# A hybrid attention and state-space encoder layer: where attention divides, where x is added, how q and k are normalized, and which token half the feed forward takes first

## The chip, the cores and the metric

The kernel runs on one core of a Trainium2 chip. The metric is the device time of one execution in microseconds (us). The kernel before took 2194.41, 2199.15 and 2200.61 us in three runs (median 2199.15).

## The reference

One encoder layer over 2048 tokens of width 1024, in float32:

```
h = rms_norm(x, norm1)
z = h @ w_in                      # 512 q, 128 k, 128 v, 512 u
q, k = rms_norm(q, q_gain), rms_norm(k, k_gain)     # over each head's 64 columns
scores = q k / sqrt(64) - slope * distance           # 128 tokens to either side
m = max(max(scores), sink);  p = exp(scores - m)
a = (p / (sum(p) + exp(sink - m))) @ v               # 8 heads, 2 kv heads
s = S5 state-space mixer of u, both directions, gelu, GLU
x = x + concat([a, s]) @ w_out
h = rms_norm(x, norm2)
out = x + square(relu(h @ w_ff1)) @ w_ff2            # 4096 wide
```

## The kernel before

Every large product is made of three TensorE matmuls of rounded high and low parts (`mm3`, L85 to L89: high × high, low × high, high × low), each 128 rows by 512 columns, into PSUM. PSUM has four tags of two banks each: `sc`, `ss`, `mm` for products and `tr` for transposes. Tokens are worked in 16 tiles of 128.

The stages, by the time in the profile: the projection of u and the set-up of the state-space part (to 134 us); the projection of q, k, v, tile by tile, with steps of the state-space part in between (to 350); attention, again with such steps (to 632, tail to 687); GLU and the output product's state-space half (to 873); the first feed-forward product (from 907 to about 1540); the second (to the end). Order in the text of the program is the programmer's; the framework's list scheduler then sets the order of instructions on each engine when the kernel is built, and each engine works its list strictly in order. All loads and stores are issued by one queue, SP, in order too.

*Norm of q and k* (`qkv_part`, L902). ScalarE squares (L918, L919), VectorE sums each of 10 heads' 64 columns (L924). Then the inverse root on 128x10 numbers: scaling (L925), ScalarE square root (L926), reciprocal (L927), one Newton step (L928 to L930, L932) and the factors `hsc` (L931). VectorE then multiplies q (L935) and twice k (L939).

*Attention* works in units: unit u is token tile n = u // 2 and kv head g = u % 2. `front(u)` makes scores and `softmax`; `back(u)`, `LEAD` units later, transposes the probabilities (`p_trans`), multiplies them with v (`pv`) and makes the attention half of the output product (`out_att`), whose result is added to x (L1100) and stored in `x1_dr`. The probabilities, 384 columns for each head, are multiplied with the reciprocal sums `rc` before they are transposed, two heads on VectorE (L1054) and two on ScalarE (L1056). S5 steps are VectorE's two-operand instructions of 512 columns (L564, L672, L675).

*Output, tiles 0 to 15* (`out_quarter`): for each tile, x1 is loaded (L1199), `out_ssm` makes two products of 512 columns (`pos`, 12 matmuls each) and adds them (L1211), x1 is stored, and `norm2` squares it on ScalarE (L1234), sums (L1235, L1236), raises to the power −1/2 on POOL (L1237) and scales it (L1238). For each pair of tiles four sums for a seven-product scheme (Strassen's) are made on POOL (L1249 to L1252), and seven pieces of 128x512 are stored in `hc_dr`.

*First feed-forward product*: 32 blocks, each seven products m = 1, 2, 6, 5, 7, 3, 4 of four `mm3`; blocks 0 to 15 take tokens 0 to 1023, blocks 16 to 31 the rest. The pieces of the token half are loaded back (`hs`, L1282), transposed (`pth`, L1292) and split into high and low (`hb`, L1293 on ScalarE, L1294 on VectorE). Weights are loaded (`w1r`, L1322), combined (L1329 to L1332) and split (`w1s`, L1338 on ScalarE, L1339 on POOL or VectorE).

Of the kernel before, what the change touches and what calls it, by code (L numbers as in the profile page):

```python
# [45 lines left out]
LEAD = 3  # L46
# [11 lines left out]
def hymba_kernel(ctx: ExitStack, tc: tile.TileContext, x, norm1, w_in, q_gain, k_gain, sink,  # L58
# [9 lines left out]

    ident = cst.tile([P, P], F32, name="ident")
    make_identity(nc, ident)  # L70
    mhalf = cst.tile([P, 16], F32, name="mhalf")
    nc.gpsimd.memset(mhalf, -0.5)

    ACT, DVE, POOL = nc.scalar, nc.vector, nc.gpsimd
    dist = cst.tile([P, 3 * P], F32, name="dist")
    nsink = cst.tile([P, NH], F32, name="nsink")
# [36 lines left out]
    v_all = att.tile([P, NT, NKV * HD], F32, name="v_all")  # L113

# [15 lines left out]
    rmag = sc.tile([P, NG], F32, name="rmag")  # L130
    dmask = sc.tile([P, GH], F32, name="dmask")
    dcol = sc.tile([64, NG // 2], F32, name="dcol")
# [267 lines left out]
    g1 = pw.tile([P, KD], F32, name="g1")  # L400
# [298 lines left out]
    def pair_out(i, h):  # L699
# [32 lines left out]
        ks = pm.tile([64, GH + C16 * GH], F32, tag="ks", name="ks")  # L732
# [154 lines left out]
    with tc.tile_pool(name="p1", bufs=2) as p1:  # L887
# [4 lines left out]
        DVE.tensor_tensor(gq[:, 0:1], gq[:, 0:1], gq[:, 1:2], op=ALU.mult)  # L892
        hsc = p1.tile([P, 10], F32, name="hsc", bufs=1)
        DVE.memset(hsc, 1.0)
        for h in range(NH):
            DVE.memset(hsc[:, h:h + 1], -1.0 / (SLOPE[h] * math.sqrt(HD)))
# [7 lines left out]
        def qkv_part(t):  # L904
# [18 lines left out]
            t3 = p1.tile([P, 10], F32, tag="t3", name="t3")  # L923
# [14 lines left out]
            for r in range(2):  # L938
                DVE.tensor_tensor(kd[:, :, r, :], pk3, rs3[:, 8:10].to_broadcast([P, 2, HD]), op=ALU.mult)  # L939
# [29 lines left out]
    with tc.tile_pool(name="pbq", bufs=2) as pbq, tc.tile_pool(name="pb", bufs=1) as pb, \  # L969
# [36 lines left out]
        mx_t = {}  # L1006
# [12 lines left out]
        def scores(n, g, h):  # L1019
# [3 lines left out]
            if h == 0:  # L1023
                p_t[n, g] = pbq.tile([P, GQ, 3 * P], F32, tag="p", name="p", bufs=LEAD + 1)
                mx_t[n, g] = pb2.tile([P, GQ], F32, tag="mx", name="mx")
# [7 lines left out]
                                     accum_out=mx_t[n, g][:, h:h + 1])  # L1033

        def softmax(n, g):
            lo, hi = keys(n)
            w = (hi - lo) * P
            mx, p = mx_t[n, g], p_t[n, g]
            ns = nsink[:, g * GQ:(g + 1) * GQ]
            nm = pb2.tile([P, GQ], F32, tag="nm", name="nm")  # L1040
            DVE.scalar_tensor_tensor(nm, mx, -1.0, ns, op0=ALU.mult, op1=ALU.min)
            es = pb2.tile([P, GQ], F32, tag="es", name="es")
            DVE.tensor_tensor(es, nm, ns, op=ALU.subtract)
            den = pb2.tile([P, GQ], F32, tag="den", name="den")
            for h in range(GQ):
                ACT.activation(out=p[:, h, 0:w], in_=p[:, h, 0:w], func=AF.Exp, bias=nm[:, h:h + 1],
                               accum_out=den[:, h:h + 1])
            ACT.activation(out=es, in_=es, func=AF.Exp)
            DVE.tensor_tensor(den, den, es, op=ALU.add)
            rc = pb2.tile([P, GQ], F32, tag="rc", name="rc")  # L1050
            DVE.reciprocal(rc, den)
# [33 lines left out]
        xr_t = {}  # L1085

        def out_att(n, half):
            if half == 0:
                xr = pb2.tile([P, D], F32, tag="xr", name="xr", bufs=1)
                nc.sync.dma_start(out=xr, in_=x2d[n * P:(n + 1) * P, :])  # L1090
                xr_t[n] = xr
            xr = xr_t[n]
# [20 lines left out]
        def front(u):  # L1113

            n, g = divmod(u, 2)
            for h in range(GQ):
# [4 lines left out]
                if h % 2 and u > 1 and wo_parts:  # L1121
# [13 lines left out]
        def back(u):  # L1135

            n, g = divmod(u, 2)
            if n < NT:
# [443 lines left out]
```

## Time and profile before

| | us |
|---|---|
| profiled execution | 2200.2 |
| its span | 2198.4 |
| runs | 2194.41, 2199.15, 2200.61 |
| TensorE busy | 2077.8 (95%) |
| VectorE busy | 1479.6 (67%) |
| ScalarE busy | 1016.0 (46%) |
| POOL busy | 590.3 (27%) |

PE is TensorE, DVE VectorE, ACT ScalarE, POOL GpSimd, SP the queue that issues transfers. A matmul counts as busy to its modelled end, and matmuls overlap, so the distance between starts is shorter than a row's duration. In 40 equal slices of the span TensorE's busy tenths are 7 in the first and one 5 near the middle of the feed forward, 9 in nearly all others; the granted clock has a 7 in the 17th and the 29th slice. The window table's columns are, after the window: its length; busy us and, in brackets, instructions of PE, of its weight loads, DVE, ACT and POOL; the mean granted clock of PE (1 is full); the share of its time that a DMA engine is busy; GB/s.

### The profile page before, as it was taken

The numbers are of one execution on the slowest core, as the hardware profiler recorded it, in microseconds if no ns is written. First come the engines' busy times: TensorE is split into PE (matmuls) and PEld (weight loads), VectorE is DVE, ScalarE is ACT, GpSimd is POOL, SyncE is SP. The second block draws the span as 40 slices with busy tenths as digits, with TensorE's granted clock in tenths as the row PEclk, the third lists the DMA queues.
The fourth block names the chain that finished last, engine by engine and source line by source line (L and its number), as shares of the span: only waits on it lengthen the run. The fifth ranks groups of instructions, "written<-read, shape, count | busy, mean of one in ns | idle before, by whom it ended". The sixth has DMA issues, their size and how long they took to land.

```text
span 2198.4 us, 30479 instructions
## 1 busy us (share of the span) xinstructions
PE 2077.8 (95%) x10546; PEld 1706.7 (78%) x10546; DVE 1479.6 (67%) x2806; ACT 1016.0 (46%) x2061; POOL 590.3 (27%) x451
## 2 busy tenths in 40 slices
PE   7999998999999997799999999999599999999999
PEld 7888886777767786688888788888487778778787
DVE  7959887998856644655445655554677776776765
ACT  4433336767666422455555655555342332333231
POOL 2000000000012223322332133221553663564441
PEclk9999999999999999799999999999799999999999
DMA  8925544333245448644445644442763443443344
GB/s 252 292 82 159 157 125 142 108 100 117 96 125 160 163 153 279 224 149 152 153 158 176 203 156 146 146 151 99 255 212 101 129 128 98 134 130 114 112 135 162
DMA packets 284394, 337.06 MB, mean 153 GB/s; under 512 B 62928, under 2 KB 211408, under 8 KB 284240
## 3 DMA queue, kind: packets, MB, share of 16 engines
q1 hardware_dynamic: 284240, 335.12, 46.9%
q8 instruction: 83, 1.36, 0.3%
q14 instruction: 71, 0.58, 0.1%
HBM read 206.11 MB, written 128.94 MB: 152 GB/s over the span
## 4 chain that ended last, share of the span: by engine, by line
PE 67%; DVE 13%; DMA 7%; POOL 5%; issue 3%; ACT 3%; SPq 1%; DVEq 0%; POOLq 0%; ACTq 0%
PE f L87 6%; PE f L89 6%; PE f L88 6%; PE f_al L89 5%; PE f_al L87 5%; PE f_al L88 5%; PE f_ga L87 3%; PE f_ga L89 3%; PE f_ga L88 3%; POOL w2s L1470 2%; PE pv L1075 1%; POOL fs L1496 1%; PE ptp L1065 1%; DVE acc L1541 1%; PE f_be L89 1%
## 5 line engine op out<-in xcount | busy, mean ns | idle before, releaser
L1541 DVE TENSOR_TENSOR acc<-f,acc 128x512 f32<-128x512 f32 x448 | 304.8, 687 | 164.6 <-PE f L89 158.0
L87 PE MATMUL f<-w2s,fs 128*128 128x512 f32 x896 | 352.9, 394 | 31.0 <-DVE acc L1541 15.7
L89 PE MATMUL f<-w2s,fs 128*128 128x512 f32 x896 | 351.4, 392 | 3.7 <-POOL fs L1496 3.7
L88 PE MATMUL f<-w2s,fs 128*128 128x512 f32 x896 | 351.3, 392 | 0.0
L1495 ACT ACTIVATE fs<-fr 128x512 fp32r<-128x512 f32 x224 | 141.6, 633 | 366.1 <-PE f L89 350.5
L1496 POOL TENSOR_TENSOR fs<-fr,fs 128x512 fp32r<-128x512 f32 x128 | 185.2, 1449 | 297.0 <-ACT fs L1495 255.8
L87 PEld LDWEIGHTS f<-w2s,fs 128*128 128x128 f32 x896 | 169.4, 189 | 74.1 <-ACT fs L1495 27.0
L1339 POOL TENSOR_TENSOR w1s<-w1r,w1s 128x512 fp32r<-128x512 f32 x96 | 135.2, 1409 | 311.9 <-ACT w1s L1338 303.0
L87 PE MATMUL f_al<-hb,w1s 128*128 128x512 f32 x512 | 201.0, 393 | 1.0 <-ACT w1s L1338 1.0
L89 PE MATMUL f_al<-hb,w1s 128*128 128x512 f32 x512 | 200.6, 392 | 1.1 <-DVE w1s L1339 0.9
L89 PEld LDWEIGHTS f<-w2s,fs 128*128 128x128 f32 x896 | 169.7, 189 | 40.3 <-POOL fs L1496 4.5
L88 PE MATMUL f_al<-hb,w1s 128*128 128x512 f32 x512 | 200.4, 391 | 0.0
L88 PEld LDWEIGHTS f<-w2s,fs 128*128 128x128 f32 x896 | 169.8, 190 | 34.7
L818 POOL TENSOR_TENSOR wgl<-wgr,wgh 128x512 fp32r<-128x512 f32 x8 | 10.4, 1311 | 521.0 <-DMA wgr<-in_w_glu_dram 508.2
L1339 DVE TENSOR_TENSOR w1s<-w1c,w1s 128x512 fp32r<-128x512 f32 x96 | 68.3, 711 | 88.0 <-ACT w1s L1338 88.0
L89 PEld LDWEIGHTS f_al<-hb,w1s 128*128 128x128 f32 x512 | 96.5, 189 | 22.0 <-DVE w1s L1339 1.3
L87 PEld LDWEIGHTS f_al<-hb,w1s 128*128 128x128 f32 x512 | 96.5, 189 | 21.3 <-ACT w1s L1338 1.4
L88 PEld LDWEIGHTS f_al<-hb,w1s 128*128 128x128 f32 x512 | 96.6, 189 | 19.6
L1338 ACT ACTIVATE w1s<-w1c 128x512 fp32r<-128x512 f32 x128 | 80.6, 630 | 49.7 <-PE f_al L89 48.4
L88 PE MATMUL f_ga<-hb,w1s 128*128 128x512 f32 x256 | 99.9, 390 | 0.0
L87 PE MATMUL f_ga<-hb,w1s 128*128 128x512 f32 x256 | 99.8, 390 | 0.0
L89 PE MATMUL f_ga<-hb,w1s 128*128 128x512 f32 x256 | 99.7, 389 | 0.0
(548 smaller groups left out, 4956.9 us busy)
## 6 DMA issues: line engine op xcount, KB each, us to landing
fr<-f_dr SPq DMA_DIRECT2D x224, 256.0 KB
w1r<-in_w_ff_dram SPq DMA_DIRECT2D x64, 512.0 KB
f_dr<-fs SPq DMA_DIRECT2D x128, 256.0 KB
f_dr<-f SPq DMA_DIRECT2D x96, 256.0 KB
w2r<-in_w_ff_dram SPq DMA_DIRECT2D x32, 512.0 KB
hs<-hc_dr SPq DMA_DIRECT2D x56, 256.0 KB
xt<-in_x_dram SPq DMA_DIRECT2D x16, 512.0 KB
q_dr<-qd SPq DMA_DIRECT2D x16, 512.0 KB
```

Of the source, the lines that this page charges most:

```text
L87: nc.tensor.matmul(ps_ap, lhsT=lh, rhs=rh, start=first, stop=False, skip_group_check=onto)
L88: nc.tensor.matmul(ps_ap, lhsT=lh, rhs=rl, start=False, stop=False, skip_group_check=onto)
L89: nc.tensor.matmul(ps_ap, lhsT=ll, rhs=rh, start=False, stop=last, skip_group_check=onto)
L818: eng_lo.tensor_tensor(lo, raw, hi, op=ALU.subtract)
L1065: nc.tensor.transpose(pt[:, h, :], p[:, h, kt * P:(kt + 1) * P], ident)
L1075: nc.tensor.matmul(po[g * HD:(g + 1) * HD, :], lhsT=v_all[:, lo + kt, g * HD:(g + 1) * HD], rhs=pT.pop((n, g, kt)), start=kt == 0, stop=kt ...
L1338: ACT.activation(out=t[:, 0], in_=src, func=AF.Copy)
L1339: (DVE if m in (6, 7, 3) else POOL).tensor_tensor(t[:, 1], src, t[:, 0], op=SUB)
L1470: (DVE if m in (6, 7, 3) and fp else POOL).tensor_tensor(t[:, 1], src, t[:, 0], op=SUB)
L1495: ACT.activation(out=t[:, 0], in_=src, func=AF.Copy)
L1496: (DVE if m in (6, 7, 3) else POOL).tensor_tensor(t[:, 1], src, t[:, 0], op=SUB)
L1541: DVE.tensor_tensor(a[:, cs], po, a[:, cs], op=ADD)
```

## The change

Seven edits. (1) Attention divides the product with v, not the probabilities: the reciprocal sums are copied to 64 columns each (`spread`), transposed on TensorE (`spread_t`, `ptr`) and multiplied into the product. The sums of both kv heads are handled at once. (2) The attention's product is stored without x; x is loaded and added when the tile is read for the state-space half (`load_xa`). (3) The inverse root of q and k is one power on POOL over 10 columns; its factors go into the scaling ahead of it. (4) The first feed-forward product begins with tokens 1024 to 2047, whose pieces are transposed straight from SBUF; only those of tokens 0 to 1023 go through `hc_dr`. Five of the last pair's seven pieces are transposed inside the first block. (5) LEAD is 2, not 3, and the output weights of the attention are split at three places in a unit, not two. (6) The squares of `norm2` go to PSUM; one of POOL's four sums goes to VectorE in the later half; the first block's weight splits are all on VectorE. (7) Small tiles are padded to 64 floats, and a tile of 24 floats is put in front.

```
-LEAD = 3
+LEAD = 2
...
+    cst.tile([P, 24], F32, name="offset")
...
+    def small(pool, n, rows=P, **kw):
+        return pool.tile([rows, 64], F32, **kw)[:, 0:n]
...
-            DVE.memset(hsc[:, h:h + 1], -1.0 / (SLOPE[h] * math.sqrt(HD)))
+            DVE.memset(hsc[:, h:h + 1], SLOPE[h] * SLOPE[h])
...
             DVE.tensor_reduce(ms, sq, axis=AX.X, op=ALU.add)
-            DVE.tensor_scalar(ms, ms, 1.0 / HD, EPS, op0=ALU.mult, op1=ALU.add)
-            ACT.activation(out=rs, in_=ms, func=AF.Sqrt)
-            DVE.reciprocal(rs, rs)
-            DVE.tensor_tensor(t3, rs, rs, op=ALU.mult)
-            DVE.tensor_tensor(t3, t3, ms, op=ALU.mult)
-            DVE.tensor_scalar(t3, t3, -0.5, 1.5, op0=ALU.mult, op1=ALU.add)
-            DVE.tensor_tensor(rs, rs, hsc, op=ALU.mult)
-            DVE.tensor_tensor(rs, rs, t3, op=ALU.mult)
+            DVE.scalar_tensor_tensor(ms, ms, HD * EPS, hsc, op0=ALU.add, op1=ALU.mult)
+            POOL.tensor_tensor(rs, ms, mhalf[:, 0:10], op=ALU.pow)
...
-            for r in range(2):
-                DVE.tensor_tensor(kd[:, :, r, :], pk3, rs3[:, 8:10].to_broadcast([P, 2, HD]), op=ALU.mult)
+            DVE.tensor_tensor(kd, pk[:, 0:128].rearrange("p (h o d) -> p h o d", o=1, d=HD).to_broadcast([P, 2, 2, HD]),
...
+        def spread(n):
+            rb_t[n] = pb.tile([P, GQ, NKV, HD], F32, tag="an", name="rb")
+            ACT.copy(rb_t[n], es_t[n].rearrange("p (g h o) -> p h g o", g=NKV, o=1).to_broadcast([P, GQ, NKV, HD]))
+
+        def spread_t(n):
+
+            pr_ = ps.tile([P, GQ, P], F32, tag="tr", name="ptr")
             for h in range(GQ):
-                if h < 2:
-                    DVE.tensor_scalar(p[:, h, 0:w], p[:, h, 0:w], rc[:, h:h + 1], None, op0=ALU.mult)
-                else:
-                    ACT.activation(out=p[:, h, 0:w], in_=p[:, h, 0:w], func=AF.Copy, scale=rc[:, h:h + 1])
+                nc.tensor.transpose(pr_[:, h, :], rb_t[n][:, h].rearrange("p g d -> p (g d)"), ident)
+            rT_t[n] = pr_
...
-            ACT.activation(out=ah, in_=pa3, func=AF.Copy)
-            DVE.tensor_tensor(al, pa3, ah, op=ALU.subtract)
+            ACT.copy(an, po.rearrange("p (h t) -> p h t", h=GQ))
+            DVE.tensor_tensor(an, an, rT_t.pop(n), op=ALU.mult)
+            ACT.activation(out=ah, in_=an, func=AF.Copy)
+            DVE.tensor_tensor(al, an, ah, op=ALU.subtract)
...
-            DVE.tensor_tensor(xr[:, cs], po, xr[:, cs], op=ALU.add)
-            if half == 1:
-                nc.sync.dma_start(out=x1_dr[n * P:(n + 1) * P, :], in_=xr)
+            xa = pb.tile([P, 512], F32, tag="xa", name="xa", bufs=2)
+            ACT.copy(xa, po)
+            nc.sync.dma_start(out=x1_dr[n * P:(n + 1) * P, cs], in_=xa)
...
+    def load_xa(n, bufs):
+
+        t = load_x1(n, po_, "x1", bufs)
+        xt = po_.tile([P, D], F32, tag="xx", name="xx", bufs=1)
+        nc.sync.dma_start(out=xt, in_=x2d[n * P:(n + 1) * P, :])
+        DVE.tensor_tensor(t, t, xt, op=ALU.add)
+        return t
...
-            junk = pn.tile([P, 512], F32, tag="junk", name="junk", bufs=1)
+            junk = ps.tile([P, 512], F32, tag="mm", name="junk")
...
-        POOL.tensor_tensor(t3, b22, b12, op=SUB)
+        (POOL if first else DVE).tensor_tensor(t3, b22, b12, op=SUB)
...
-    early = right_operands(0, [(m, i) for i in range(4) for m in PRODUCTS])
-    for n, _ in enumerate(out_quarter(3)):
-        if n > 0:
-            for _ in range(7):
-                next(early, None)
+    x1 = load_xa(NT // 2, 2)
+    pend = None
+    for n in range(NT // 2, NT):
+        nx = load_xa(n + 1, 2) if n + 1 < NT else None
+        out_ssm(n, x1)
+        if n == 11:
+            sb_stack.close()
+        nc.sync.dma_start(out=x1_dr[n * P:(n + 1) * P, :], in_=x1)
+        if pend is not None:
+            for m in PRODUCTS:
+                trans(m, (n - NT // 2) // 2 - 1, pend[m])
+        if n == NT - 1:
+            for j, m in enumerate((1, 2)):
+                trans(m, 3, h2_t[n - 1][:, j * 512:j * 512 + 512])
+        pend = norm2(n, x1)
+        x1 = nx
...
+            for m in PRODUCTS[2:6]:
+                trans(m, 3, pend[m])
+                after(next(blk))
+            trans(4, 3, pend[4])
```

On VectorE, in the projection of q, k, v, one tile's norm of q and k stands among S5 steps. Before, from the sum of squares to the split of q:

```order
L924 TENSOR_REDUCE msq<-sq 128x10
L564 TENSOR_TENSOR tmp<-bb_r,pv_n 128x512
L925 TENSOR_SCALAR msq<-msq 128x10
L564 TENSOR_TENSOR q_r<-c_r,pw_r 128x512
L564 TENSOR_TENSOR v<-v,tmp 128x512
L927 RECIPROCAL rsq<-rsq 128x10
L564 TENSOR_TENSOR tmp<-ta_s,tb_s 128x512
L928 TENSOR_TENSOR t_1977<-rsq 128x10
L564 TENSOR_TENSOR q_n<-c_n,pw_r 128x512
L929 TENSOR_TENSOR t_1977<-t_1977,msq 128x10
L931 TENSOR_TENSOR rsq<-rsq,hsc 128x10
L564 TENSOR_TENSOR t_c<-t_c,tmp 128x512
```

Now, the same tile:

```order
L931 TENSOR_REDUCE msq<-sq 128x10
L571 TENSOR_TENSOR tmp<-bb_r,pv_n 128x512
L932 SCALAR_TENSOR_TENSOR msq<-msq,hsc 128x10
L571 TENSOR_TENSOR q_r<-c_r,pw_r 128x512
L571 TENSOR_TENSOR v<-v,tmp 128x512
L936 TENSOR_TENSOR sq<-pq,rsq 128x512
L939 TENSOR_TENSOR kd<-pk,rsq 128x256
L571 TENSOR_TENSOR tmp<-ta_s,tb_s 128x512
L943 TENSOR_TENSOR qd<-sq,qd 128x8x64
```

The multiplication of q (L936) now stands two S5 steps behind the step that feeds POOL's power (L932), and seven small steps are one.

On SP, the queue of all transfers, in the output product's tiles 8 to 15. Before, `x` is a tile of the sum, `hc_dr` takes pieces for the first feed-forward product and `hs` are those loaded back:

```order
L1254 DMA hc_dr<-t_9277 128x512
L1199 DMA x_9289<-x_dr 128x1024
L1261 DMA x_dr<-x_9158 128x1024
L1282 DMA hs<-hc_dr 128x512 x4
L1261 DMA x_dr<-x_9289 128x1024
L1282 DMA hs<-hc_dr 128x512 x6
L1246 DMA hc_dr<-h_9383 128x512
L1282 DMA hs<-hc_dr 128x512 x4
```

Now, the last three tiles and what follows them (`xx` is a tile of the input x):

```order
L1229 DMA xx<-in_x_dram 128x1024
L1222 DMA x_9058<-x_dr 128x1024
L1350 DMA x_dr<-x_8965 128x1024
L1229 DMA xx<-in_x_dram 128x1024
L1222 DMA x_9109<-x_dr 128x1024
L1350 DMA x_dr<-x_9058 128x1024
L1350 DMA x_dr<-x_9109 128x1024
L1370 DMA w1r<-in_w_ff_dram 128x4x256 x6
```

No store to `hc_dr` and no load from it stands between the last eight tiles and the weights `w1r` any more; a load of the input stands with each tile.

## Rows read from the trace of the kernel before

**Rows 1.** Windows, stage by stage: columns as told above.
```profile
133.70:350.10 216.40, 202.51 (x1374) 175.06 (x1372) 195.48 (x450) 74.33 (x209) 1.11 (x11) 0.99 0.44 135
350.10:384.20 34.10, 26.29 (x157) 20.64 (x157) 24.52 (x87) 28.02 (x73) 0.00 (x0) 0.90 0.58 166
384.20:632.00 247.80, 242.88 (x1550) 186.24 (x1549) 212.11 (x581) 174.93 (x467) 0.00 (x0) 1.00 0.33 104
687.00:814.60 127.60, 123.36 (x529) 99.94 (x528) 70.78 (x95) 51.45 (x91) 35.79 (x30) 0.99 0.47 155
814.60:907.00 92.40, 69.06 (x306) 53.84 (x304) 43.56 (x70) 29.77 (x63) 24.93 (x24) 0.84 0.75 255
935.00:1182.00 247.00, 247.00 (x1092) 204.58 (x1091) 127.49 (x183) 137.51 (x234) 70.95 (x53) 1.00 0.45 152
```
**Rows 2.** Chain of waits to the feed forward: start us, us, what.
```profile
867.96 0.44 PE pth L1292 x4
868.87 0.23 PE pos__9407 L87
...
869.79 0.24 PE pos__9407 L89
...
871.07 6.49 DMA x<-x_dr
...
880.14 0.16 DVE ss L1236
...
880.44 0.56 POOL ss L1237
881.02 1.28 DVE h L1238
...
886.63 4.60 DMA hs<-hc_dr
...
893.71 0.42 SPq L1247
...
901.15 5.11 DMA w1r<-in_w_ff_dram
```
**Rows 3.** TensorE's timeline: start, us, instruction, count, idle before and releaser.
```profile
879.71 1.94 PE L1292 MATMUL pth<-ident,hs 128*128 128x128 f32 x8 [6.69 <-DMA hs<-hc_dr]
...
906.99 0.79 PE L87 MATMUL f_al<-hb,w1s 128*128 128x512 f32 x1 [1.03 <-ACT w1s L1338]
```
**Rows 4.** VectorE's groups, 137 to 348: count, busy us, mean ns, idle before.
```profile
L564 DVE TENSOR_TENSOR v<-bb_r,pv_r 128x512 f32<-128x512 f32 x10 | 6.8, 684 | 17.2 <-DMA u_dr<-ut 17.2
```
**Rows 5.** Chain of waits, 210 to 221 (VectorE bound): start, share, what.
```profile
215.28 0.08 DVE msq L925
...
215.96 0.13 DVE rsq L927
...
217.23 0.16 DVE t L929
...
217.97 0.17 DVE rsq L932
...
219.47 0.39 DVE kd L939 x2
219.86 0.40 DVE k_ll L950
```
**Rows 6.** Chain of waits, 830 to 857: a load of x.
```profile
851.01 4.55 DMA x<-x_dr
```
**Rows 7.** Timelines of VectorE and POOL, 829.5 to 837.5.
```profile
831.62 0.69 DVE L1211 TENSOR_TENSOR x<-pos__9032,x 128x512 f32<-128x512 f32 x1 [1.09 <-PE pos__9032 L89]
833.16 0.90 DVE L1235 TENSOR_TENSOR ss<-ss 128x1 f32<-128x1 f32 x1 [0.85 <-ACT junk L1234]
...
832.75 1.29 POOL L1251 TENSOR_TENSOR t<-h 128x512 f32<-128x512 f32 x1
```
**Rows 8.** VectorE's groups, 357 to 687.
```profile
L1054 DVE TENSOR_SCALAR p<-p,rc 128x384 f32<-128x384 f32 (+1 forms) x64 | 24.0, 416 | 0.4
```

More of the change, by code (lines that the diff above doesn't have):

```diff
@@ L113, in hymba_kernel @@
     v_all = att.tile([P, NT, NKV * HD], F32, name="v_all")
+    dist = att.tile([P, 3 * P], F32, name="dist")
+    nsink = small(att, NH, name="nsink")
     raw_h = att.tile([P, NKV * S], F32, tag="kh", name="raw_h")
@@ L129, in hymba_kernel @@
     tb_s = sc.tile([P, NG, 16], F32, name="tb_s")
-    rmag = sc.tile([P, NG], F32, name="rmag")
-    dmask = sc.tile([P, GH], F32, name="dmask")
-    dcol = sc.tile([64, NG // 2], F32, name="dcol")
+    rmag = small(sc, NG, name="rmag")
+    dmask = small(sc, GH, name="dmask")
+    dcol = small(sc, NG // 2, 64, name="dcol")
     KEEP, SCRATCH = 352, 1536
@@ L399, in hymba_kernel @@
     wql = pw.tile([P, KD, 768], F32R, name="wql")
-    g1 = pw.tile([P, KD], F32, name="g1")
+    g1 = small(pw, KD, name="g1")
     hstack = ExitStack()
@@ L1024, in scores @@
                 p_t[n, g] = pbq.tile([P, GQ, 3 * P], F32, tag="p", name="p", bufs=LEAD + 1)
-                mx_t[n, g] = pb2.tile([P, GQ], F32, tag="mx", name="mx")
+                if g == 0:
+                    for d, nm in ((mx_t, "mx"), (nm_t, "nm"), (den_t, "den"), (es_t, "es")):
+                        d[n] = pb2.tile([P, NH], F32, tag=nm, name=nm, bufs=3)
             qs = q_spl[n, g]
@@ L1120, in front @@
                 yield 0.33
-                if h % 2 and u > 1 and wo_parts:
+                if h and u > 1 and wo_parts:
                     split_wo(*wo_parts.pop(0))
@@ L1137, in back @@
             n, g = divmod(u, 2)
+            if g == 1 and n < NT:
+                sums(n)
             if n < NT:
@@ L1140, in back @@
                     p_trans(n, g, kt)
+                    if g == 1 and kt == 0:
+                        spread(n)
                     yield 0.44
@@ L1230, in norm2 @@
         h2_t[n] = h2
[L1231 removed]
+        ss = small(pn, 2, tag="ss2", name="ss2", bufs=2)
         for i in range(2):
[L1233 removed]
+            junk = ps.tile([P, 512], F32, tag="mm", name="junk")
             ACT.activation(out=junk, in_=x2[:, i * 512:i * 512 + 512], func=AF.Square, accum_out=ss[:, i:i + 1])
@@ L1245, in norm2 @@
         t4 = pn.tile([P, 512], F32, tag="t4", name="t4")
-        nc.sync.dma_start(out=hc_dr[n // 2, 1], in_=b11)
-        nc.sync.dma_start(out=hc_dr[n // 2, 2], in_=b21)
-        nc.sync.dma_start(out=hc_dr[n // 2, 3], in_=b22)
-        POOL.tensor_tensor(t3, b22, b12, op=SUB)
+        first = n < NT // 2
+        if first:
+            for m, t in ((1, b11), (2, b21), (3, b22)):
+                nc.sync.dma_start(out=hc_dr[n // 2, m], in_=t)
+        (POOL if first else DVE).tensor_tensor(t3, b22, b12, op=SUB)
         POOL.tensor_tensor(b12, b12, b11, op=SUB)
@@ L1252, in norm2 @@
         POOL.tensor_tensor(t4, b21, t2, op=SUB)
-        for m, t in ((5, b12), (6, t2), (7, t3), (4, t4)):
-            nc.sync.dma_start(out=hc_dr[n // 2, m], in_=t)
+        if first:
+            for m, t in ((5, b12), (6, t2), (7, t3), (4, t4)):
+                nc.sync.dma_start(out=hc_dr[n // 2, m], in_=t)
+        return {1: b11, 2: b21, 3: b22, 5: b12, 6: t2, 7: t3, 4: t4}
     def out_quarter(q):
-        x1 = load_x1(4 * q, po_, "x1", 2)
+        x1 = load_xa(4 * q, 2)
         for n in range(4 * q, 4 * q + 4):
-            nx = load_x1(n + 1, po_, "x1", 2) if n % 4 < 3 else None
+            nx = load_xa(n + 1, 2) if n % 4 < 3 else None
             out_ssm(n, x1)
@@ L1352, in keep @@
     def keep(g, m, t):
-        nc.sync.dma_start(out=f_dr[g % NFB, g // NFB, m], in_=t)
+        nc.sync.dma_start(out=f_dr[g % NFB, 1 - g // NFB, m], in_=t)
     def cell(tag, bufs=1):
-        return pf.tile([P, 512], F32, tag=tag, name=tag, bufs=bufs)
+        return pc.tile([P, 512], F32, tag=tag, name=tag, bufs=bufs)
     def ff1_block(g):
@@ L1408, in hymba_kernel @@
     load_w1(1)
+    left_w1(0, (1, 2))
+    for m in (1, 2):
+        split_w1(0, m)
     left_w1(0)
-    for m in PRODUCTS:
+    for m in PRODUCTS[2:]:
         split_w1(0, m)
@@ L1415, in hymba_kernel @@
         blk = ff1_block(g)
-        switch = right_operands(1, [(m, i) for m in PRODUCTS for i in range(4)]) if g == NFB - 1 else None
+        switch = right_operands(0, [(m, i) for m in PRODUCTS for i in range(4)]) if g == NFB - 1 else None
         def after(m, g=g, switch=switch):
@@ L1425, in hymba_kernel @@
         next(blk)
+        if g == 0:
+            next(blk)
         if g + 1 < NG1:
@@ L1433, in hymba_kernel @@
             load_w1(g + 2)
-        for _ in range(5):
-            after(next(blk))
+        if g == 0:
+            after(2)
+            for m in PRODUCTS[2:6]:
+                trans(m, 3, pend[m])
+                after(next(blk))
+            trans(4, 3, pend[4])
+            pnb_stack.close()
+            ph_ = d1_stack.enter_context(tc.tile_pool(name="ph_", bufs=1))
+        else:
+            for _ in range(5):
+                after(next(blk))
         last = (blk, after)
```

90 lines of the change are left out of this document (47 added, 43 removed).

## The prediction

> **What bounds the kernel now.** I read the window table first. Three kinds of stretch stand in it [rows 1]. In the feed forward TensorE is the bound without a gap: 1092 matmuls of 512 columns in 247.00 us, 0.2262 us each. In the attention (384.2 to 632) it is busy 242.88 of 247.80 us, with VectorE at 212 and ScalarE at 175. In the q, k, v projection (133.7 to 350.1) VectorE is the bound: 195.48 us busy of 216.40, and one row of its waits, 17.2 us for the load of u at the stretch's start [rows 4], fills nearly all of the rest; TensorE has 216.40 − 202.51 = 13.9 us idle, which is all that this stretch can give back.
>
> The weak place is between the attention and the feed forward. From 814.6 to 907 TensorE is busy 69.06 of 92.40 us at a mean granted clock of 0.84 [rows 1]; the output product's last matmul stands at 869.79 and the first feed-forward matmul at 906.99 [rows 2, 3]. The chain of waits says why [rows 2]: load of x (6.49 us), norm, store of its sums to HBM, load back (4.60), transposes, the issue (0.42) and landing of the next stores, load of w1 (5.11). One wait for the loads back is 6.69 us long on TensorE [rows 3].
>
> **The change part by part.** The sum is made against the profiled execution, 2200.2 us; its span is 2198.4. That is 1.05 us above the median 2199.15 of the runs shown, which I take off at the end. Minus is time saved.
>
> *Second half before first (814.6 to 907.0, 92.4 us).* Removed: the 28 stores and 28 loads of the half that comes first, and the queueing of x loads behind them. Added: for each of the 8 tiles a second load (the input x) and an addition over 1024 columns. None like it is in the rows; an addition of 512 takes 0.69 [rows 7] and the norm's product of 1024 takes 1.28 [rows 2], so I take 1.3. Work of a pair of tiles: TensorE 48 output matmuls × 0.233 (the mean of the 0.23 and 0.24 of [rows 2]) = 11.2 and 28 transposes × 0.11 (0.44 for four [rows 2]) = 3.1, so 14.3. VectorE: 2 × (1.3 + two additions 1.4 + small 0.3 + norm 1.28) + 7 subtractions of hb × 0.69 + one sum of 0.69 = 14.1. The buffer of x: two of them, so each carries every second tile through load 4.55 [rows 6], issue 0.42, the new addition 1.3, one addition 0.7, then from the load's landing to the end of the norm 4.7, which holds the other addition (877.56 to 882.30 [rows 2]): 11.7. VectorE and TensorE thus set about 14, and they wait on each other through two PSUM banks, which the squares of the norm now use as well. I take 15.5: 1.2 more for one handover of VectorE per tile, 0.6 each, about one more two-operand step of 512 columns (0.69 [rows 7]) ahead of the one awaited. Four pairs: 62. From the last output matmul to the first feed-forward one: w1's new tiles lie where the output weights lay, so their load cannot start earlier: a store's issue and its own, 0.42 each, load 5.11, copy to w1s and handovers about 1, 7.0; beside it the last addition and norm 4.7, eight transposes 0.9 to 1.94 [rows 3], and the copy and subtraction of hb 1.3, about 7.6. I take 7.6. Twenty transposes of the last pair are left over inside the first block: 2.2. Together 71.8 against 92.4: **−21**. Ends: pair at 14.1 and no further wait, −27; pair at 19 (rival 1), −6.6. The first feed-forward block now makes four subtractions on VectorE that POOL made; VectorE has half of that stretch free (127.49 of 247 [rows 1]), so nothing.
>
> *Norm of q and k (16 tiles).* Removed are a scaling, a ScalarE root, a reciprocal and five more steps on 10 columns. What a small step costs VectorE is its share of the chain, not its duration: 0.08, 0.13, 0.16 and 0.17 for the four shown, three more at 0.08 [rows 5], 0.78 in all. One step of 0.08 to 0.16 takes their place: 0.66 saved, 16 × 0.66 = 10.6. The two copies of k of 128 columns (0.39) become one of 256; the 256-column step in the rows takes 0.40: nothing. Added is a power on POOL. On one column it takes 0.56, and from the end of the step before it (880.30) to the norm that waits (881.02) 0.72 pass [rows 2]. In the new order one or two steps of 0.60 stand between, so between nothing and 0.72 is uncovered: 0 to 11.5, half is 5.8. Net **−5**. Lower end −13.9 (TensorE's idle time). Upper end: if ten columns cost ten times one, 5.6 per tile, less two covering steps 1.2, less 0.66 saved: 16 × 3.74 = +60 (rival 3). Queued behind the wait on VectorE is the whole S5 work of this stretch, and TensorE's products of it behind that.
>
> A row speaks against part of this: the small sum at 833.16 took 0.90 and ended when POOL's subtraction ended at 834.04, while the addition at 831.62, which reads PSUM, took its usual 0.69 beside POOL [rows 7]. The Trainium skill, SBUF — State Buffer, section "Who interferes with whom", says that a VectorE instruction with two SBUF inputs and a GpSimd one that reads SBUF exclude each other for a whole instruction; the trace agrees in these rows. By the rule each power would hold up VectorE for its 0.56 whatever stands between, 16 × 0.56 = 9.0, and this term would be −1.6 instead of −5.
>
> *Attention.* VectorE loses 64 scalings of 0.416 [rows 8], 32 additions of 0.69 and half of its small steps, and gains 16 products of 0.69: 26.6 + 22 − 11 = 38; ScalarE loses the other 64 scalings and gains 64 copies (two for each of 16 token blocks, 32 of the result), about as much. TensorE, the bound, gets 64 transposes × 0.11 = 7.0. Body: +7.0 from these, less what it waits for VectorE: 4.9 idle, and more that the table cannot show, as a matmul counts as busy to its modelled end. I take +1; ends +7 (nothing is waited for less) and −12 (half of VectorE's 38 us comes off, 19 − 7). Fill (350.1 to 384.2): 7.8 us idle, ScalarE 28.02 of 34.10; it loses its scalings and a table load, and one unit less is looked ahead: half, −4. Together **−3**, ends +7 and −16.
>
> *x added later, in tiles 0 to 7:* eight additions of 1.3 on VectorE, 70.78 busy of 127.60 [rows 1]: hidden; without that cover 10.4. The second load per tile, 4 MB, comes at a DMA share of 0.47: hidden.
>
> *Tiles moved onto a common grid of 256 bytes.* Output matmuls stand 0.233 apart, feed-forward ones of the same shape 0.2262 [rows 1, 2]. If the place of the operand is the reason, 192 matmuls of tiles 0 to 7 give 1.3, and the projections, whose operands move likewise, some 2: **−3**, ends 0 and −10.
>
> Feed forward from 935 on: TensorE without a gap, same matmuls: 0.
>
> Sum: −21 − 5 − 3 − 3 = −32; 2200.2 − 32 − 1 = **2167 us**.
>
> **Rivals.** (1) *The load chain or POOL sets the pace of tiles 8 to 15.* For it: loads of 4.55 and 6.49 us [rows 2, 6], and POOL's three sums of 1.3 and two powers of 0.56 per pair, 5.0, which hold up VectorE's two-SBUF steps [rows 7]: 14.1 + 5.0 = 19 a pair, the stretch 85.8, −6.6. Against: fewer transfers than now, and additions from PSUM are not held up. Time 2181 (2172 to 2194).
> (2) *The waits of TensorE on VectorE go with VectorE's work.* For it: in the attention VectorE has 38 us less of 212, and in the projection TensorE's 13.9 us idle are all its waiting on VectorE. Attention −16, projection −14, the other terms as above: 2145 (2137 to 2153). Against: TensorE at 98% busy there, with 7 us more to do.
> (3) *The power on ten columns is slow.* Place: POOL, once a tile, VectorE behind it. Price up to 5.6 us a tile, +60 where −5 stood: 2232. It eats the other 27 us from a power of 3.6 us on (3.6 − 1.2 − 0.66 = 1.74, × 16 = 28). For it: POOL's one power takes as long as 40% of a 512-column sum. Against: a 512-column sum at 1.29 is 2.5 ns a column, so that nearly all of the 0.56 seems to be a fixed cost.
>
> **How the numbers follow.** Forecast 0.55 (own range 2153 to 2175), rival 1 0.16, rival 2 0.19, rival 3 0.10. About 0.3% (6.6 us) is what a measurement of this kernel can tell from no change. Faster: 0.55 + 0.19 + 0.13 of rival 1 = 0.87; same: 0.03 of rival 1 and 0.03 of rival 3 = 0.06; slower: the rest of rival 3, 0.07. The range leaves out the slow end of rival 3 and the fast third of rival 2: 2140 to 2192.
>
> **What would show it.** Right: the first feed-forward matmul some 8 us after the last output matmul instead of 37 (869.79 to 906.99 [rows 2, 3]); pairs of tiles 8 to 15 near 15.5 us apart; a ten-column power below 0.8 us; VectorE's busy time in the projection some 10 us less, and that stretch about 5 shorter; attention within 4 us of 247.8; output matmuls 0.2262 apart; feed forward as long as before. Wrong: TensorE waiting for loads of x between tiles (rival 1), the attention shorter by 10 or more (rival 2), power rows of microseconds (rival 3); or, for the sum as a whole, transposes of the probabilities' divisors holding a PSUM bank for which other transposes wait.

## The result, and the profile after

The changed kernel takes 2231.05 us (median of 4 runs, 2229.08 to 2232.6) against 2199.8 before: a ratio of 1.0147, 95% interval 1.0129 to 1.0165: slower by 31 us. The forecast was 2167 and faster. The profiled execution of the changed kernel has a span of 2227.3 us.

The window table of the changed kernel, taken between the same events as before (columns as ahead of the prediction):

```profile
134.00:368.20 234.20, 207.12 (x1372) 179.14 (x1371) 185.93 (x338) 69.90 (x192) 36.90 (x27) 0.97 0.44 125
368.20:398.80 30.60, 25.53 (x149) 20.86 (x149) 20.72 (x63) 22.39 (x62) 0.00 (x0) 0.80 0.52 152
398.80:724.00 325.20, 308.81 (x1863) 225.80 (x1861) 217.09 (x539) 215.11 (x539) 13.83 (x10) 1.00 0.28 86
724.00:856.90 132.90, 126.49 (x534) 101.24 (x533) 80.61 (x103) 52.70 (x94) 39.27 (x30) 0.97 0.59 195
856.90:932.70 75.80, 59.86 (x293) 47.84 (x291) 53.35 (x79) 26.77 (x60) 21.36 (x20) 0.94 0.48 164
960.00:1207.00 247.00, 247.00 (x1092) 204.51 (x1091) 130.77 (x184) 137.64 (x234) 71.99 (x53) 1.00 0.45 154
```

and the row of before for the whole attention, from its first to its last output matmul, to set beside the third:

```profile
384.20:680.80 296.60, 287.07 (x1767) 216.53 (x1766) 238.97 (x637) 207.96 (x540) 11.70 (x9) 0.99 0.37 116
```

Read by length, stage for stage: the projection of q, k, v 216.4 to 234.2, although VectorE's busy time fell from 195.48 to 185.93 [rows 1]; the fill 34.1 to 30.6; the attention 296.6 to 325.2; tiles 0 to 7 133.8 to 132.9; tiles 8 to 15 and the way to the feed forward 92.4 to 75.8; the feed forward's matmuls as dense as before. So +18, −3, +29, −1, −17, and 3 in the rest: +29 in the traces.

**The projection.** One tile on VectorE, and POOL's instruction in it (start, us, instruction, idle before and releaser):

```profile
222.27 0.16 DVE L932 SCALAR_TENSOR_TENSOR msq<-msq,hsc 128x10 f32<-128x10 f32 x1
222.35 0.68 DVE L571 TENSOR_TENSOR x_i<-yi,t_c 128x512 f32<-128x512 f32 x1
224.88 0.69 DVE L936 TENSOR_TENSOR sq<-pq,rsq 128x512 f32<-128x512 f32 x1 [1.85 <-POOL rsq L933]
```

```profile
222.58 2.27 POOL L933 TENSOR_TENSOR rsq<-msq,mhalf 128x10 f32<-128x10 f32 x1 [15.64 <-DVE msq L932]
...
234.12 1.95 POOL L933 TENSOR_TENSOR rsq<-msq,mhalf 128x10 f32<-128x10 f32 x1 [9.27 <-DVE msq L932]
```

The power takes 1.95 us in the four tiles where no step of VectorE is in progress when it starts (the second row is one), 2.27 to 2.32 in the eleven where a step of 512 columns is, and 2.80 in the one where a step of 1.2 us is. The order shown ahead of the prediction, two S5 steps between L932 and L936, is that of the first tile alone: in eleven tiles one S5 step stands between, in four none. Then VectorE stands still, for 1.25 us in the first tile and 1.79 to 2.13 us in the others. Over the stage, by VectorE's waits (waited for: us in total, times, longest):

```profile
DVE sq L936 <- POOL rsq L933: 30.0, 16, 2.1
DVE v L571 <- DMA u_dr<-ut: 17.2, 1, 17.2
...
```

The second of these is as long before, and most of it lies ahead of the stage.

**The attention.** TensorE's waits with a releaser, of the changed kernel, then of before over the same stretch:

```profile
PE ptp L1079 <- ACT pT L1081: 7.5, 6, 1.8
PE pglu L92 <- ACT yh L854: 2.7, 1, 2.7
PE pkd L733 <- ACT xa L1113: 2.1, 1, 2.1
PE poa L92 <- ACT ah L1099: 2.1, 3, 1.1
...
```

```profile
PE pv L1075 <- DVE xr L1100: 3.9, 1, 3.9
PE ptp L1065 <- ACT pT L1067: 3.1, 4, 1.4
PE poa L89 <- DVE al L1082: 1.3, 2, 0.8
PE pkd L726 <- DVE xr L1100: 1.0, 1, 1.0
...
```

Before, most waits name VectorE (6 of 9.5 us); now they name ScalarE (15 of 16.4 us). VectorE lost 22 us of work in this stretch (238.97 to 217.09), ScalarE gained 7 (207.96 to 215.11). Of the 29 us that the stretch is longer, 7 are such waiting; TensorE's busy time grew by the other 22 (287.07 to 308.81), of which some 5 are GLU matmuls that were done in tiles 0 to 7 before.

**The way to the feed forward.** One wait holds most of what is left idle there, TensorE's for POOL's third sum of a pair:

```profile
PE pth L1329 <- POOL t L1284: 13.6, 4, 7.3
```

### The profile page after: what moved, and what is told of

It reads as the page before. It is cut to its first block, busy times and chain, and to the rows that moved or that the text cites. A ratio compares the mean times of both kernels' runs of the same rounds, so it can differ in the third digit from the quotient of the medians.

```text
span 2227.3 us, 30316 instructions
## 1 busy us (share of the span) xinstructions
PE 2092.9 (94%) x10610; PEld 1711.8 (77%) x10610; DVE 1460.6 (66%) x2590; ACT 1009.3 (45%) x2027; POOL 620.2 (28%) x459
## 4 chain that ended last, share of the span: by engine, by line
PE 44%; DVE 5%; POOL 4%; issue 2%; DMA 2%; ACT 0%; SPq 0%; DVEq 0%; POOLq 0%; ACTq 0%
PE f L92 6%; PE f L94 6%; PE f L93 6%; PE f_al L93 5%; PE f_al L92 5%; PE f_al L94 5%; PE f_ga L93 2%; POOL w2s L1535 2%; PE f_ga L94 2%; PE f_ga L92 2%; POOL fs L1561 2%; DVE acc L1606 1%; PE f_be L93 1%; PE f_be L94 1%; PE f_be L92 1%
## 5 line engine op out<-in xcount | busy, mean ns | idle before, releaser
L92 PE MATMUL f<-w2s,fs 128*128 128x512 f32 x896 | 353.0, 394 | 31.6 <-DVE acc L1606 16.6
L1390 POOL TENSOR_TENSOR w1s<-w1r,w1s 128x512 fp32r<-128x512 f32 x93 | 130.4, 1402 | 300.4 <-ACT w1s L1389 287.5
L1036 DVE CUSTOM_DVE_ANT_0 p<-pss,dist 128x384 f32<-128x384 f32 (+1 forms) x128 | 67.0, 537 | 63.4 <-PE pss L1035 59.7
L93 PE MATMUL f_ga<-hb,w1s 128*128 128x512 f32 x256 | 100.1, 391 | 1.5 <-DVE hb L1331 1.5
L92 PE MATMUL f_ga<-hb,w1s 128*128 128x512 f32 x256 | 99.9, 390 | 0.0
```

The lines of the kernel that those rows point to most:

```text
L92: nc.tensor.matmul(ps_ap, lhsT=lh, rhs=rh, start=first, stop=False, skip_group_check=onto)
L93: nc.tensor.matmul(ps_ap, lhsT=lh, rhs=rl, start=False, stop=False, skip_group_check=onto)
L1036: DVE.tensor_tensor_reduce(out=p_t[n, g][:, h, 0:w], in0=pss, in1=dist[:, off:off + w], scale=-SLOPE[g * GQ + h], scalar=-3.0e38, op0=ALU. ...
L1390: (DVE if m in (6, 7, 3) or g == 0 else POOL).tensor_tensor(t[:, 1], src, t[:, 0], op=SUB)
```

## The experiments

The stages are taken between the same events in each run: B is the projection of q, k, v; C the fill, the attention and tiles 0 to 7 together (work moves between these three: the changed kernel does some of the GLU's matmuls earlier); D tiles 8 to 15 up to the first feed-forward matmul; E the first feed-forward product from its first to its last matmul. Times are medians of the runs, stages us of the profiled execution.

| kernel | time | B | C | D | E |
|---|---|---|---|---|---|
| before | 2200 | 216.4 | 464.4 | 92.4 | 630.7 |
| changed | 2231.0 | 234.4 | 488.7 | 75.8 | 632.2 |
| 1 changed, norm undone | 2212.1 | 221.0 | 489.1 | 75.5 | 632.6 |
| 2 changed, division undone | 2221.2 | 233.8 | 481.6 | 78.7 | 631.1 |
| 3 changed, x undone | 2218.1 | 233.0 | 482.0 | 74.9 | 631.8 |
| 4 before, power alone | 2211.0 | 230.1 | 466.1 | 92.5 | 629.4 |
| 5 before, feed-forward order alone | 2202.4 | 217.2 | 467.6 | 74.6 | 648.0 |
| 6 changed, 1 to 3 together | 2192.4 | 217.8 | 473.5 | 74.6 | 629.8 |
| 7 as 1, with an idle power | 2212.0 | 219.5 | 489.6 | 76.4 | 630.4 |
| 8 changed, divisors in other bank | 2229.2 | 235.6 | 492.5 | 75.5 | 632.6 |
| 9 as 5, moved by 32 bytes | 2187.9 | 218.2 | 467.6 | 74.6 | 630.3 |
| 10 as 9, sums on VectorE | 2187.9 | 216.8 | 468.1 | 71.3 | 631.5 |
| 11 as 9, look-ahead 2 | 2192.5 | 219.4 | 473.1 | 74.7 | 630.1 |
| 12 changed, divisors not transposed | 2221.8 | 234.2 | 477.8 | 76.2 | 631.1 |
| 13 as 9, weights split at three places | 2192.0 | 218.5 | 470.4 | 74.6 | 632.0 |

**1. The norm undone.**

```
...
-            DVE.scalar_tensor_tensor(ms, ms, HD * EPS, hsc, op0=ALU.add, op1=ALU.mult)
-            POOL.tensor_tensor(rs, ms, mhalf[:, 0:10], op=ALU.pow)
+            DVE.tensor_scalar(ms, ms, 1.0 / HD, EPS, op0=ALU.mult, op1=ALU.add)
+            ACT.activation(out=rs, in_=ms, func=AF.Sqrt)
...
```

> The changed kernel with the norm of q and k made as before (square root on ScalarE, reciprocal, Newton step on VectorE), everything else changed. Theory 1: the ten-column power takes about 2 us and VectorE stands still for 1.9 of them in each of 16 tiles, 30 us, against 10 us of small steps saved: the projection of q, k, v goes back from 234 to about 216 us and the time from 2231 to about 2212. Rival 1: the projection is longer for another reason (the new places of the tiles, the order of the S5 steps); then it stays above 228 and the time above 2225.

Measured 2212.07, ratio to before 1.0054 (1.0039 to 1.0069): 19 us come back, 13 of them in B by the traces. Theory 1 holds for the time and not for all of the stage: B falls to 221.0, not to the 216 expected.

```profile
134.00:355.00 221.00, 205.59 (x1375) 178.76 (x1373) 195.22 (x434) 74.68 (x209) 1.11 (x11) 0.97 0.46 133
```

VectorE is as busy as before (195.22 us to 195.48), but idle for 5 us more, and TensorE's granted clock is 0.97 where it was 0.99. What makes these 5 us is not shown.

**4. The power alone.** The opposite edit, made in the kernel before.

> The kernel before with one part of the change alone: the norm of q and k by one power on POOL. Theory 1: 16 waits of 1.9 us on VectorE less 10 us of steps saved: about 2218, 18 to 20 above before. Rival 1: the wait appears only in the changed kernel's order; then 2190 to 2205.

Measured 2210.99, 1.0052 (1.0036 to 1.0069): +11, with B +13.6. The direction of theory 1, less than its size: by itself the power costs 11 us, within the changed kernel 19, and no run shows why these differ. VectorE waits as long here as in the changed kernel; the groups of VectorE and of POOL in this run:

```profile
L928 DVE TENSOR_TENSOR sq<-pq,rsq 128x512 f32<-128x512 f32 x16 | 11.1, 692 | 30.0 <-POOL rsq L925 30.0
```

```profile
L925 POOL TENSOR_TENSOR rsq<-msq,mhalf 128x10 f32<-128x10 f32 x16 | 35.8, 2236 | 188.3 <-DVE msq L924 178.3 <-DVE t L661 10.0
```

**7. The power without the wait.** The kernel of run 1, with one instruction more, whose result nobody reads:

```
             DVE.tensor_scalar(ms, ms, 1.0 / HD, EPS, op0=ALU.mult, op1=ALU.add)
+            xp = p1.tile([P, 10], F32, tag="xp", name="xp")
+            POOL.tensor_tensor(xp, ms, mhalf[:, 0:10], op=ALU.pow)
             ACT.activation(out=rs, in_=ms, func=AF.Sqrt)
```

> The changed kernel with the norm of q and k made as before, and POOL's ten-column power issued as well, its result unused. It tells waiting for the power apart from sharing a port with it. Theory 1: only the wait costs; the time is that of the kernel with the norm undone, 2212, within 4. Rival: the power holds up VectorE while it runs (1.95 us, 16 times); then 2220 or above.

Measured 2211.95, as without it (2212.07). POOL's power is as long, and VectorE's multiplication of q waits for nothing:

```profile
L935 POOL TENSOR_TENSOR xp<-msq,mhalf 128x10 f32<-128x10 f32 x16 | 35.9, 2242 | 177.9 <-DVE msq L933 167.9 <-DVE t L668 10.0
```

```profile
L945 DVE TENSOR_TENSOR sq<-pq,rsq 128x512 f32<-128x512 f32 x16 | 11.0, 686 | 0.5
```

Nor does the power hold up VectorE's other steps. One tile's power (start, us, instruction), and a step of VectorE with both inputs in SBUF that began and ended beside it:

```profile
173.77 2.26 POOL L935 TENSOR_TENSOR xp<-msq,mhalf 128x10 f32<-128x10 f32 x1 [10.73 <-DVE msq L933]
```

```profile
174.26 0.63 DVE L571 TENSOR_TENSOR tmp<-yr,t_s 128x512 f32<-128x512 f32 x1
```

In this run 15 such steps began while a power ran: 0.685 us in the median, the same as the others. Only the wait costs.

**2. The division undone.** `softmax` and the end of `pv` as before, for each kv head:

```
...
-            ACT.copy(an, po.rearrange("p (h t) -> p h t", h=GQ))
-            DVE.tensor_tensor(an, an, rT_t.pop(n), op=ALU.mult)
-            ACT.activation(out=ah, in_=an, func=AF.Copy)
-            DVE.tensor_tensor(al, an, ah, op=ALU.subtract)
+            ACT.activation(out=ah, in_=pa3, func=AF.Copy)
+            DVE.tensor_tensor(al, pa3, ah, op=ALU.subtract)
...
```

> The changed kernel with the probabilities divided before they are transposed, as before; look-ahead 2, x added later and the power stay. Theory 2: in the attention the 64 transposes of the divisors cost TensorE 8 us, and their PSUM bank and the two more copies on ScalarE make other transposes wait for some 10 more: the stretch from the first to the last attention output matmul goes from 325 to about 305 and the time from 2231 to about 2212. Rival 2: look-ahead 2 or the copies of the result on ScalarE make the waits; then only the 8 us of the transposes return and the time stays at 2221 or above. Rival 2b: more work on VectorE again makes it slower still, 2231 or above.

Measured 2221.18, 1.0093 (1.0075 to 1.0111): 10 us. The attention alone is 310.3, 15 shorter, but 5 of these are GLU matmuls that move back to tiles 0 to 7 and 3 stand in the fill; C keeps 7.1. Half of theory 2's gain, and by the expectation's own line it is rival 2's result, if only just (2221 was its edge): TensorE's 8 us and little more.

**12. The divisors not transposed.** `spread_t` gives the copy itself, in a buffer of its own, to the multiplication, so the attention's result is another one.

```
...
-            pr_ = ps.tile([P, GQ, P], F32, tag="tr", name="ptr")
-            for h in range(GQ):
-                nc.tensor.transpose(pr_[:, h, :], rb_t[n][:, h].rearrange("p g d -> p (g d)"), ident)
-            rT_t[n] = pr_
+            rT_t[n] = rb_t[n].rearrange("p h g d -> p h (g d)")
```

> The changed kernel without the 64 transposes of the divisors: the product is multiplied with the untransposed copy, so the attention's result is another one; all copies on ScalarE and the multiplication on VectorE stay. Theory 2: the attention falls by the 8 us of TensorE and a few of the waits for the bank, 2220 to 2224. Rival: the cost is in the longer chain of copies between the product and the next (ScalarE, VectorE, ScalarE, VectorE); then it falls by less than 4, to 2227 or above.

Measured 2221.82, 1.009 (1.0058 to 1.0121): 9 us, as much as undoing the whole division. The attention's row:

```profile
398.20:712.90 314.70, 300.36 (x1801) 218.63 (x1800) 212.47 (x531) 212.96 (x537) 13.24 (x10) 1.00 0.29 87
```

TensorE's busy time falls by 8.4 us, its idle time only from 16.4 to 14.3: the 64 transposes are the division's price mostly by their own time, and little by making others wait. What the copies and the longer chain cost is less than this can tell; the interval is 7 us to either side.

**8. The divisors in another bank.** `tag="tr"` becomes `tag="mm"` for `ptr`.

> The changed kernel with the transposed divisors in the PSUM tag of the output products, not in that of the transposes. Theory 2: the divisors hold a transposes' bank for up to 5 us while the next transposes wait; freed, TensorE's waits at the transposes of the probabilities fall from 8 us to below 4 and the attention by 5 to 10: 2221 to 2226. Rival: the transposes wait because ScalarE's copies stand behind its exponentials; then the time stays within 4 of 2231.

Measured 2229.18 (2226.98 to 2231.42), 1.0132 (1.0114 to 1.0149): within 4 us of 2231, as the rival says, and no different from the changed kernel that the runs can tell. TensorE's waits at the transposes of the probabilities did fall, from 7.5 to 2.0 us, but those at the output products rose from 2.1 to 6.4:

```profile
PE poa L92 <- ACT ah L1099: 6.4, 5, 1.9
PE ptp L1079 <- ACT pT L1081: 2.0, 4, 0.9
```

Both waits are for ScalarE; the bank changed which product waits. That the order of ScalarE's list makes them is read from these rows; no run changed that order alone.

**3. x undone.**

```
...
-            ACT.copy(xa, po)
-            nc.sync.dma_start(out=x1_dr[n * P:(n + 1) * P, cs], in_=xa)
+            DVE.tensor_tensor(xr[:, cs], po, xr[:, cs], op=ALU.add)
+            if half == 1:
+                nc.sync.dma_start(out=x1_dr[n * P:(n + 1) * P, :], in_=xr)
...
```

> The changed kernel with x added to the attention's output product on VectorE and stored whole, as before, and no second load in the later tiles. Theory 2: the attention stays within 5 us of 325, and tiles 0 to 15 of the output product gain 3 to 6 us from the additions and loads they lose: about 2226. Rival 3: the 32 copies of the result on ScalarE, in front of the copies that free the transposes' banks, make the attention's waits: then the attention falls by 10 or more and the time to 2215 or below.

Measured 2218.11, 1.0077 (1.0062 to 1.0092): 13 us, more than theory 2 gave. The attention falls by 3.4 (321.8), tiles 0 to 7 by 2.9, tiles 8 to 15 by 0.9, the projection by 1.4; 2 to 4 are spread over the rest. In C TensorE is idle 4 and busy 3 us less. Neither theory: a little everywhere, and by which way is not shown.

**5 and 9. The feed-forward order alone, and 32 bytes.** Everything but edits 4 and 6 as before, except that three small tiles have other places or sizes (`dist`, `nsink`, `ks`); then one line more:

```
+    cst.tile([P, 8], F32, name="offset")
     ident = cst.tile([P, P], F32, name="ident")
```

> The kernel before with one part of the change alone: the second token half first, its pieces transposed from SBUF, the squares in PSUM (look-ahead 3, probabilities divided, x added in the attention, norm of q and k as before, tiles not padded). Theory 4: this part saves by itself what the traces show between the last eight tiles' first output matmul and the first feed-forward one (92.4 to 75.8): about 17, less the loads of x that it does not need, 2181 to 2184. Rival 4: the gain needs the other parts, or is given back in the feed forward; 2192 or above.

> The kernel with the feed-forward order alone, with one tile of 8 floats put in front, which moves the left tiles by 32 bytes: the split weights w1s and the transposed tokens hb then have the same address modulo 256 (224; without it 192 and 224). Theory 5: the place of the two operands to each other sets the pace, 0.2262 us a matmul instead of 0.233, and the first feed-forward product falls from 648 to 631: 2183 to 2186. Rival 5: the slower pace comes from something else in that kernel; then it stays at 2202.

Measured 2202.41 (1.0005, 0.9994 to 1.0015), then 2187.87 (0.9941, 0.9918 to 0.9964). In the first, D gives 17.8 and E takes 17.3 back: in 247 us only 1061 matmuls pass. In the second, 1091. The windows, of 5 and of 9:

```profile
920.00:1167.00 247.00, 247.00 (x1061) 198.40 (x1059) 123.75 (x175) 133.24 (x227) 68.27 (x52) 1.00 0.45 151
```

```profile
920.00:1167.00 247.00, 247.00 (x1091) 204.66 (x1091) 130.88 (x185) 137.74 (x235) 71.36 (x52) 1.00 0.45 153
```

TensorE is busy all the time and at full clock in both; each matmul is 0.2328 or 0.2264 us. The one line moves tiles and does nothing else. In the built programs it changes where the weights stand to the tokens: addresses modulo 256 of 192 and 224 in 5, 224 and 224 in 9. So theory 5 holds, and it is the two together that count and not the one address: in kernel 5 the output matmuls, both operands at 192, follow each other every 0.227 us, before (224 and 32) every 0.234 (medians). Kernel 9 is faster than the kernel before and the changed one.

**6. Three parts undone.**

> The changed kernel with the norm, the division and the addition of x all made as before; look-ahead 2, the output weights split at three places, the padded tiles and the new feed-forward order stay. Theory: the three parts add up, 2231 less 19, 10 and 13 as each gave alone: 2189, and what stays above the kernel with the new feed-forward order alone is the look-ahead of 2, 5 to 10 us in the attention. Rival: look-ahead 2 costs nothing; then both kernels come out within 3 us.

Measured 2192.37, 0.9962 (0.9949 to 0.9975), 3 above the sum, as the theory says. It is 4.5 above kernel 9, which is not clear of the noise; C is 5.9 above that of kernel 9.

**11 and 13. Look-ahead 2, and the weights at three places.**

```
-LEAD = 3
+LEAD = 2
...
-                if h % 2 and u > 1 and wo_parts:
+                if h and u > 1 and wo_parts:
```

> The moved kernel with the feed-forward order alone, with look-ahead 2 and the output weights split at three places in a unit. Theory 6: look-ahead 2 shortens the fill by 3 us and costs the attention 8 to 12 by more changes between kinds of product and waits behind ScalarE: 4 to 9 us slower than with look-ahead 3. Rival 6: it costs nothing, within 2 us, and the 11 us that the attention keeps with all three parts undone come from the places of the tiles.

> The moved kernel with the feed-forward order alone, look-ahead 3 again, but the attention's output weights split at three places in a unit instead of two. It tells apart the two edits that the kernel with look-ahead 2 needed together. Theory 6: the look-ahead itself costs the 14 us of the attention; the time is that of the kernel without this edit, 2188, and the attention 296 to 299. Rival: the weights' splits, moved up in front of ScalarE's and VectorE's work of the first units, cost it; then the attention is 305 or more and the time 2191 or above.

Measured 2192.51 with both edits and 2191.95 with the second alone, both against 2187.87 (whose runs go from 2184.87 to 2192.58). By time the two cannot be told apart: the second alone has the time of its rival and the attention of theory 6. By the traces the attention is 310.3 with both and 299.0 with the second alone, against 296.4; the fill 28.8, 34.3 and 34.4. So look-ahead 2 lengthens the attention by 11 and gives 6 back in the fill and 3 in tiles 0 to 7: net 2.7 in C, beside 2.8 of the splits. With the same number of matmuls in C, TensorE is busy 444 us in kernel 9, 445 with the splits and 452 with look-ahead 2 as well, and idle 23, 25 and 21: look-ahead 2 saves waits and loses more in busy time. Changes between kinds of product (last section) go from 118 to 139 in C, which is about 2 of those us; the rest is not explained. That the expected 4 to 9 us belong to the look-ahead is not shown.

**10. POOL's sums on VectorE.** `POOL` becomes `POOL if first else DVE` for the other three sums of `norm2`.

> The same, and in the later token half the three sums that POOL still makes are made on VectorE. TensorE waits 13 us for POOL's sums there in the changed kernel. Theory: a sum takes 0.7 instead of 1.3 to 1.7 and the stretch before the feed forward falls by 4 to 8 us: 2177 to 2182. Rival: VectorE is the bound of these tiles and takes it back; within 3 us of the kernel without it.

Measured 2187.91: the rival. D falls by 3.3 in the trace, TensorE now waits for VectorE's sums (8.6 us where it waited 11.9 for POOL's), and the time is that of kernel 9, to the 5 us that these intervals leave open (0.9946, 0.9925 to 0.9967):

```profile
PE pth L1316 <- DVE t L1271: 8.6, 4, 6.1
```

## Why the prediction was wrong

It failed in three terms of its sum: the cover of the power, VectorE's relief set against TensorE's new work in the attention, and x's move, which it held to be hidden. The parts, as undoing them one by one priced them: norm 19 (11 when made alone, run 4), x 13, division 10, look-ahead and splits 5 (kernels 11 and 9), less 12 that the feed-forward order saves (kernel 9): +35, against +31 measured together.

**The norm (−5; B measured +18, of which undoing the norm returns 13 and the norm alone adds 14).** The saved small steps were right: 10.6 forecast, VectorE's busy time fell by 9.6. What failed is the cover: "between nothing and 0.72 is uncovered", from the row of a power over one column. Ten columns take 1.95 us and more instead of 0.56, at most one S5 step covers it in 15 of the 16 tiles, and 1.9 stay bare in the mean: 30.0. This is rival 3's mechanism and I had the upper end in hand, 5.6 a tile. I set it aside because a subtraction over 512 columns costs 2.5 ns a column; a power is another operation, and that row said nothing of it. By the rows now, 1.39 us for nine columns more are some 154 ns a column, an estimate. That rival 3's time, 2232, is the measured one is chance: at 2 us the power was below the 3.6 from which rival 3 alone would decide. The rule of the Trainium skill (SBUF — State Buffer, section "Who interferes with whom") would have put the term at −1.6, with VectorE held by each power. The traces agree in one direction only: a power issued while a step of VectorE ran took 2.27 instead of 1.95, so POOL was held; in run 7 VectorE's steps that began during a power took their usual 0.685 and were not.

**The attention and fill (−3, measured +25; +24 with tiles 0 to 7).** I booked 7 us of transposes and then let VectorE's relief pay for them: 38 us less work, of which 6 were to come back. The work fell by 22, and TensorE's waits for VectorE did fall, from 6 us to 1; but its waits for ScalarE rose from 3 to 15, so that nothing was paid. I had counted ScalarE's work ("about as much") and not where its copies now stand, between one product and the next. The transposes cost 9 of the time and 11 in C (run 12), the look-ahead and splits 5 together (run 11), and x's move cost 7 in C (run 3), which I had priced at nothing in the attention and "hidden" in tiles 0 to 7; all of it together was 13, and by which way is open. Another 3 in C come with the new feed-forward order, in tiles 0 to 7 (kernel 9), which I had not seen at all. That is 26 where the stages say +24. The forecast's last sentence named divisors that hold a PSUM bank; in run 8 another bank gave back 2 us, which is within the spread, so that place is not the cost.

**Tiles 8 to 15 (−21, measured −16.6).** Right in mechanism: 75.8 against 71.8. What is late next is not the load of x but POOL: transposes wait 13.6 us for its third sum (one of POOL's sums took 1.29 in [rows 7]; this one takes 1.51 on average now). From the last output matmul (921.8) to the first of the feed forward 10.9 us pass, not 8, of them 7.3 waiting for that sum. Run 10 shows that moving the sums to VectorE mostly moves the wait: 3.3 us less in D, none in the time.

**The places of the tiles (−3).** The rows had it, 0.233 against 0.2262 [rows 1, 2], and the output matmuls did go to 0.227; with tiles 0 to 7 only 0.9 shorter, the gain is not seen in the sum. But the size at stake was larger than my 10: E has 2688 matmuls, and with the feed-forward order alone, without edit 7, each was 0.0064 longer, 17 us (kernels 5 and 9). I had not asked what the new order does to the places of its own tiles.

**Two slips that changed nothing in the sum.** VectorE's wait of 17.2 us for u does not fill its idle time in the projection. It ends at 136.45 and so lies almost wholly ahead of the stretch, which begins at 133.7:

```profile
136.45 0.69 DVE L564 TENSOR_TENSOR v<-bb_r,pv_r 128x512 f32<-128x512 f32 x1 [17.16 <-DMA u_dr<-ut]
```

Only 2.8 of VectorE's 20.9 idle us there are this wait; 14 are waits for TensorE and ScalarE, so VectorE was less of a bound than I said. And pairs of tiles at 14.1 would have ended at −26, not at −27.

## What to carry to other kernels

A step handed to another engine costs the engine that waits the whole length of the step less what really stands between the two in its list; where no row shows that operation at that width, the upper bound belongs in the sum as a case and not in a tail. Relief of an engine pays for new work on the bounding one only by what the bounding one waits for it (6 us here), and only if no other engine's wait takes its place: look where the moved work stands in the new engine's list, not only at how much it is. After any change in the layout, compare the distance between starts of matmuls of one shape: a busy engine at full clock can still be 3% slower.

## What the runs showed of the hardware

- A power on POOL over 128x10 takes 1.95 us, over 128x1 0.55 to 0.60.
- A power over 128x10 that starts while VectorE runs a step with two inputs from SBUF takes longer (2.27 to 2.32 us); such steps of VectorE that start while a power runs do not (0.685 us in the median, run 7).
- In the first feed-forward product matmuls of 128x512 follow each other every 0.2264 us where the two operands have the same address modulo 256, and every 0.2328 where they differ (192 and 224; one tile of 32 bytes tells them apart, kernels 5 and 9). Whether 256 is the number that counts was not tried. Equal places are not enough everywhere: the attention's output matmuls of the changed kernel have both operands at 224 and still follow each other every 0.231 us in the median.
- A product of rounded operands that follows a transpose or another float32 product starts its successor later. In the changed kernel's attention, on TensorE (start, us):

```profile
547.99 0.34 PE L1035 MATMUL pss<-k_ll,qs 128*128 128x384 f32 x1
548.16 0.60 PE L1079 MATMUL ptp<-ident,p 128*128 128x128 f32 x4
548.52 0.42 PE L1034 MATMUL pss<-k_hh,qs 128*128 128x384 f32 x1
548.78 0.34 PE L1035 MATMUL pss<-k_ll,qs 128*128 128x384 f32 x1
548.95 0.34 PE L1034 MATMUL pss<-k_hh,qs 128*128 128x384 f32 x1
549.13 0.34 PE L1035 MATMUL pss<-k_ll,qs 128*128 128x384 f32 x1
```

The score product behind the transposes takes 0.26 to the next, those behind other score products 0.17; over the whole stretch the medians are 0.260 and 0.174. The attention before has 107 such changes, the changed one 140: 33 × 0.1, some 3 us of its 29.
